# RWKV rounds of a hybrid decoder layer: three preparation steps asked for at other places of the round, and ten small operations per round moved to ScalarE

## The chip, the cores and the metric

The kernel runs on one core of a Trainium2 chip. A core has TensorE for matrix products (PE in the rows, with its weight loads as PEld), VectorE (DVE), ScalarE (ACT), GpSimd (POOL) and SyncE (SP), which issues the DMAs. Each engine works through its own queue in order; the engines wait for one another by semaphores. The metric is the device time of one execution in microseconds (us), the median of several runs; lower is better.

## The reference

A decoder layer for one sequence of 1024 positions and width 1024: RWKV-7 time mixing with 16 heads of 64, beside a dilated attention; then a cross-attention to 256 memory rows, a squared-ReLU MLP and norms. The change is in the RWKV part:

```
r, w, k, v, a_, b_ = ...            # projections of the normed input, mixed with the position before
for t in range(SEQ):                # per head, state is 64 x 64
    sa = state @ a_t
    state = state * w_t + outer(sa, b_t) + outer(v_t, k_t)
    y_t = state @ r_t
yn = groupnorm(y) * gn_w + gn_b
bonus = sum(r * k * r_k, per head) * v
out = (yn + bonus) * g
```

with `a_ = -kk`, `b_ = kk * a`, `k = p_k * (1 + (a - 1) * k_a)`, and `kk` the per-head normalised key.

## The kernel before

**Pairs, halves and chunks.** The 16 heads are worked off as 8 pairs p, a pair filling the 128 partitions. The 1024 positions are two halves of 512, a half is 8 chunks of 64 positions. Within a chunk the recurrence is put in closed form: a triangular system per chunk and head is solved, and what remains from chunk to chunk is a short scan over the state Z.

**Steps for one pair.** Each is a Python generator whose `yield`s cut it into small pieces:
- `proj`: the dense products (128x128 weights against 128x512 inputs, each value split into a high and a low part, three products per pair) that give r, k, v, evacuated by `shiftmix`.
- `prep_a` (L462): decay sums (L483), exponentials (L490, L491), the normalised key (L496 to L499), `ta` scaled by L502 on GpSimd, then k times ta (L503).
- `prep_b`: the operands `ar`, `bk` of the chunk products, and the chunk products themselves, masked into A (L546).
- `prep_d` (L550): `bk` times the decay of the chunk (L557, one instruction of 1024 elements), V centred and turned by TensorE into `pvt`, copied to UV by two half copies (L564 on ScalarE, L565 on VectorE), and b and k turned into BK (L571, L572).
- `prep_e` (L575): 64 small products of A with V, copied to UV (L582).
- `prep_c` (L585): the bonus: r times k (L588), the sum over a head by `block_sum` (L440, L442 and two products), times v (L594), and gn_b added by L595 on GpSimd.
- `solve` (L602): the triangular systems in blocks of 16: transposes (L613), then 14 times a product (L620) and a sum (L622) of tiny extent on VectorE, each needing the one before, and a last pair of transposes into DD (L633).
- `solve_pe` (L636): the joining products. From DD, four sets of small products double the solved blocks, from 16 to 32 to 64. Each set takes two PSUM banks and is read by VectorE or ScalarE (L648, L657, L666, L674, L684) before the next can begin.
- `post` (L688): the chunk matrices for the scan; its copies are L713 on ScalarE and L714 on VectorE for the two head halves of WT, L719 on ScalarE, and L726, ScalarE for the first head and VectorE for the second.
- `scan` (L745): chunk by chunk, a product into `pz`, Z made from it by VectorE (L760), a product into `pY`. `gnorm` (L765) follows.

All the small products' results lie in a pool of four PSUM banks (`pms`); the dense ones have two banks of their own.

**The order.** A round handles scan and group norm of pair p, the steps from prep_b to post of pair p+1, and proj and prep_a of pair p+2, with gate products as further dense work. `weave` merges the generators: every stream has a window (t0, t1) on a scale from 0 to 100 and a count n, and its pieces are written at t0 + (i + 1/2)(t1 - t0)/n, the earliest first. The windows of rounds 0 to 7 stand in W (L786), those of the round before them in W0. Where this text says "due", it means this place. The gate's dense pieces have dues 2.6 to 39.4, those of proj 43.2 to 98.8 in a round with both. From that written order the tile framework makes the queue of every engine when it compiles, along with all waits; the queue need not have the written order.

**The helper lines.** L125 is the product helper `mm`, so it is the line of nearly all small products: they are told apart by their tiles (`pz`, `pvt`, `psb`, `ps` for the joining products, `po` for those of prep_e and post). L143 to L145 are the dense products. L110 and L112 split the dense weights, on ScalarE and GpSimd.

Of the kernel before, what the change touches and what calls it, by code (L numbers as in the profile page):

```python
# [11 lines left out]
AF = mybir.ActivationFunctionType  # L12
ALU = mybir.AluOpType
# [28 lines left out]
def hybrid_layer(ctx, tc, x, mem, norm_mix_g, w_in, shift_mu, w0, w2, a0, a2, g2, k_k, k_a, r_k, gn_w, gn_b,  # L42
# [230 lines left out]
    with tc.tile_pool(name="ra", bufs=1, side="right", reuse_waits="tile") as ra, \  # L273
# [188 lines left out]
        def prep_a(p, half):  # L462
            d = st[p]
            hs = slice(half * H2, (half + 1) * H2)
            r, k, v = [d["rkv"][half].get(x) for x in "rkv"]
            wah = d["wa"]
            d[half] = e = {}
            psw = pms.tile([P, H2], F32, tag="m", name=nm("psw"))
            psa = pms.tile([P, H2], F32, tag="m", name=nm("psa"))
            mm(psw, wah[:, 0, :], WD[:, hs], True, False)  # L470
            mm(psa, wah[:, 1, :], AD[:, hs], True, False)
            mm(psw, wal[:, 0, :], WD[:, hs], False, True)
            mm(psa, wal[:, 1, :], AD[:, hs], False, True)
            sc = r3.tile([P, 2, H2], F32, tag="t4", name=nm("sc"), bufs=2)
            e["sg"], cs = sg, cs = sc[:, 0, :], sc[:, 1, :]
            nc.scalar.activation(sg, psw, AF.Tanh, bias=hw0[:, p:p + 1], scale=0.5)
            tt = r3.tile([P, 2, H2], F32, tag="t3", name=nm("ta"), bufs=2)
            ta, e["kk"] = tt[:, 0, :], tt[:, 1, :]
            sq = e["kk"]
            nc.scalar.activation(ta, psa, AF.Tanh, bias=ha0[:, p:p + 1], scale=0.5)  # L480
            yield
            nc.vector.tensor_scalar_add(sg, sg, 1.0)
            nc.vector.tensor_tensor_scan(cs, smask, sg, 0.0, op0=ALU.mult, op1=ALU.add)  # L483
            nc.scalar.activation(sq, k, AF.Square, scale=vc(V_KK, p))
            yield
            pss = pms.tile([P, H2], F32, tag="m", name=nm("pss"))
            block_sum(pss, sq)
            yield
            e["G"] = G = r3.tile([P, H2], F32, tag="t2", name=nm("G"), bufs=2)
            nc.scalar.activation(G, cs, AF.Exp, scale=-0.5 * CDEC)  # L490
            nc.scalar.activation(cs, cs, AF.Exp, scale=0.5 * CDEC)  # L491
            e["Gi"] = cs
            yield
            kk = sq
            nc.vector.tensor_scalar_max(kk, pss, 1e-24)
            nc.scalar.activation(kk, kk, AF.Ln, scale=2.0 ** 20)  # L496
            nc.scalar.activation(kk, kk, AF.Exp, bias=l2b, scale=-0.5)
            yield
            nc.vector.scalar_tensor_tensor(kk, k, vc(V_KK, p), kk, op0=ALU.mult, op1=ALU.mult)  # L499
            nc.vector.scalar_tensor_tensor(sg, ta, 1.0, cs, op0=ALU.add, op1=ALU.mult)  # L500
            yield
            nc.gpsimd.tensor_scalar(ta, ta, hka[:, p:p + 1], omhka[:, p:p + 1], op0=ALU.mult, op1=ALU.add)  # L502
            nc.vector.tensor_tensor(k, k, ta, op=ALU.mult)  # L503
            yield

# [44 lines left out]
        def prep_d(p, half):  # L550
            d = st[p]
            e = d[half]
            v = d["rkv"][half].get("v")
            bk, gC = e["bk"], e["gC"]
            us, vs = rows(half)

            nc.vector.tensor_tensor(bk, bk, gC.unsqueeze(3).broadcast_to([P, 8, 2, CH]), op=ALU.mult)  # L557
            e["UV"] = UV = rb.tile([P, 8, P], F32, tag="UV", name=nm("UV"), bufs=2)
            pvt = pms.tile([P, 4, P], F32, tag="m", name=nm("pvt"))
            for q in range(4):  # L560

                mm(pvt[:, q, :], v[:, q * P:(q + 1) * P], cen)
            uvp = UV.rearrange("p (q e) f -> p q e f", e=2)
            nc.scalar.copy(uvp[vs, :, 0, :], pvt[0:64])  # L564
            nc.vector.tensor_copy(uvp[vs, :, 1, :], pvt[64:128])  # L565
            yield
            e["BK"] = BK = rb.tile([P, 8, P], F32, tag="BK", name=nm("BK"), bufs=2)
            for q in range(2):
                pb = pms.tile([P, 4, P], F32, tag="m", name=nm("pb"))
                for i in range(4):  # L570
                    nc.tensor.transpose(pb[:, i, :], bk[:, q * 4 + i, :, :], ident)  # L571
                nc.scalar.copy(BK[:, q * 4:q * 4 + 4, :], pb)  # L572
                yield
# [11 lines left out]
        def prep_c(p, half):  # L585
            d = st[p]
            r, k, v = [d["rkv"][half].get(x) for x in "rkv"]
            nc.vector.scalar_tensor_tensor(r, r, vc(V_RK, p), k, op0=ALU.mult, op1=ALU.mult)  # L588
            yield
            psb = pms.tile([P, H2], F32, tag="m", name=nm("psb"))  # L590
            block_sum(psb, r)
            yield
            d[half]["bv"] = bv = rb.tile([P, H2], F32, tag="bv", name=nm("bv"), bufs=3)
            nc.vector.tensor_tensor(bv, psb, v, op=ALU.mult)  # L594
            nc.gpsimd.tensor_scalar(bv, bv, 1.0, vc(V_GB, p), op0=ALU.mult, op1=ALU.add)  # L595
            yield

        def quads():
# [89 lines left out]
        def post(p):  # L688


            d = st[p]
            Am = d["Am"]
            ar, UV, BK, gC = [[d[half][x] for half in range(2)] for x in ("ar", "UV", "BK", "gC")]
            d["S"] = rA.tile([P, 2, 4, 8, CH], F32, tag="A", name=nm("S"))
            St = d["S"]
            for f in range(2):
                nc.gpsimd.tensor_tensor(St[:, f, 0], id2.broadcast_to([P, 8, CH]), gC[f].broadcast_to([P, 8, CH]),
                                        op=ALU.mult)

            def us(f):  # L700
                return rows(f)[0]

            def am(f, c, h):
                return Am[us(f), 16 * f + 2 * c + h, 0:64]

            WT = []
            for f in range(2):
                pt = pms.tile([P, 4, P], F32, tag="m", name=nm("paT"))
                for q in range(4):
                    nc.tensor.transpose(pt[:, q, :], d[f]["ara"][:, 0, 2 * q:2 * q + 2, :], ident)  # L710
                WT.append(r3.tile([P, 8, P], F32, tag="bk", name=nm("WT"), bufs=2))
                wtp = WT[f][us(f)].rearrange("p (q e) f -> p q e f", e=2)
                nc.scalar.copy(wtp[:, :, 0, :], pt[0:64])  # L713
                nc.vector.tensor_copy(wtp[:, :, 1, :], pt[64:128])  # L714
            yield
            pu = four(lambda f, c, h, hh: (am(f, c, h), UV[f][us(f), c, hh]))
            for f in range(2):
                for hh in heads():
                    nc.scalar.copy(UV[f][us(f), :, hh], pu[f][hh])  # L719
            yield  # L720
            pw = four(lambda f, c, h, hh: (am(f, c, h), WT[f][us(f), c, hh]))

            for f in range(2):
                Wm = Am[us(f), 16 * f:16 * f + 16, 0:64].rearrange("p (c h) t -> p c h t", h=2)
                for h, hh in enumerate(heads()):
                    (nc.vector.tensor_copy if h else nc.scalar.copy)(Wm[:, :, h, :], pw[f][hh])  # L726
            yield
            ps = four(lambda f, c, h, hh: (BK[f][:, c, hh], UV[f][:, c, hh]))
            for f in range(2):
                nc.scalar.copy(St[:, f, 2], ps[f])  # L730
            yield
            ps = four(lambda f, c, h, hh: (am(f, c, h), BK[f][us(f), c, hh]))
            for f in range(2):
                nc.vector.tensor_tensor(St[:, f, 0], St[:, f, 0], ps[f], op=ALU.add)
            yield
            ps = four(lambda f, c, h, hh: (am(f, c, h), Am[us(f), 16 * f + 2 * c + h, 64:128]))
            for f in range(2):
                nc.vector.tensor_tensor(St[:, f, 1], ar[f][:, :, 1, :], ps[f], op=ALU.add)
            yield
            ps = four(lambda f, c, h, hh: (UV[f][:, c, hh], Am[:, 16 * f + 2 * c + h, 64:128]))  # L740
            for f in range(2):
                nc.scalar.copy(St[:, f, 3], ps[f])
            yield
# [21 lines left out]
        def gnorm(p, half):  # L765
# [17 lines left out]
            nc.sync.dma_start(yscr[p * P:(p + 1) * P, half * H2:(half + 1) * H2], y)  # L783
            yield

        W = dict(s0=(0, 22), s1=(23, 46), g0=(24, 36), g1=(47, 60), b0=(0, 10), b1=(7, 17), so=(17, 36), d0=(20, 30),  # L786
                 d1=(28, 38), sp=(36, 54), c0=(40, 44), c1=(45, 49), e=(37, 39), po=(56, 82), a0=(62, 78), a1=(76, 94))
        W0 = dict(b0=(20, 29), b1=(28, 37), so=(37, 52), d0=(38, 45), d1=(44, 51), sp=(52, 66), c0=(50, 54), c1=(54, 58),
                  e=(50, 52), po=(68, 90), a0=(68, 82), a1=(80, 96))
        GD = [4, 1, 1, 1, 1, 1, 1, 4, 2]  # L790
# [937 lines left out]
```

## Time and profile before

| | us |
|---|---|
| median of 3 runs (lowest, highest) | 2441.41 (2440.43, 2444.42) |
| the profiled execution | 2439.77 |
| its span, first instruction to last | 2438.1 |

The profile is of one execution on the chip. All places in the rows are us from the start of its span. The RWKV part lies before 915 us; the rounds with W begin at about 221, 319.4, 414.5, 509.1, 605.5, 702 and 796.5, and the last, with no preparation, at 883. A row of a timeline gives start, length, engine, line, operation, output tile <- input tiles, shapes, and how many instructions it merges; what stands in brackets is the idle time of that engine just before it and what ended it.

### The profile page before, as it was taken

What the parts mean: (1) busy time and instruction counts of PE and PEld (TensorE: products, weight loads), DVE (VectorE), ACT (ScalarE), POOL (GpSimd) and SP (SyncE); (2) the same over time, 40 slices, a digit from 0 to 9 for tenths busy, and PEclk for the clock granted to TensorE, in tenths of its full rate; (3) what the DMA queues carried; (4) which work ended last, traced back from release to release, by engine and by line L of the source; (5) the groups of instructions that cost most, each with busy time, mean ns of one, the idle gap of its engine ahead of it and who ended that gap; (6) DMA issues with size and microseconds to landing.
All of it is one profiled execution on the core that took longest, in us unless ns stands there. A gap on an engine that the chain in (4) does not pass through costs nothing. (4 is left out here: it accounts for less than half of the span.)

```text
span 2438.1 us, 46897 instructions
## 1 busy us (share of the span) xinstructions
PE 2304.0 (95%) x18645; PEld 1834.2 (75%) x18645; DVE 1589.6 (65%) x2723; ACT 1046.3 (43%) x2032; POOL 922.5 (38%) x749
## 2 busy tenths in 40 slices
PE   6999999999999999999999999999889999899997
PEld 5777777777777777777678888887668887677775
DVE  6638677686786612232555664456799999797785
ACT  5525645645456434334433454444422223344344
POOL 4321222222222222111245535324555554565664
PEclk9999999999999999999999999999999999999998
DMA  4221111111111123121355553223244445554342
GB/s 171 57 64 34 37 39 34 37 43 34 37 33 33 49 70 102 40 69 41 90 176 157 163 153 115 68 60 91 65 143 156 151 155 178 160 168 124 114 133 75
DMA packets 301618, 226.73 MB, mean 93 GB/s; under 512 B 16229, under 2 KB 252375, under 8 KB 301399
## 3 DMA queue, kind: packets, MB, share of 16 engines
q1 hardware_dynamic: 301111, 223.20, 30.2%
q8 instruction: 147, 2.41, 0.4%
q14 instruction: 72, 0.59, 0.1%
q10 hardware_dynamic: 288, 0.52, 0.1%
HBM read 169.99 MB, written 53.67 MB: 92 GB/s over the span
## 5 line engine op out<-in xcount | busy, mean ns | idle before, releaser
L143 PE MATMUL acc<-ah,wh 128*128 128x512 f32 (+1 forms) x1600 | 652.2, 408 | 11.3 <-DVE h L1048 3.0
L144 PE MATMUL acc<-al,wh 128*128 128x512 f32 (+1 forms) x1600 | 618.3, 386 | 3.2 <-POOL al L231 1.9
L145 PE MATMUL acc<-ah,wl 128*128 128x512 f32 (+1 forms) x1600 | 618.1, 386 | 0.4 <-POOL wl L112 0.4
L112 POOL TENSOR_TENSOR wl<-wr,wh 128x512 fp32r<-128x512 f32 x248 | 334.5, 1350 | 708.5 <-ACT wh L110 665.5
L143 PEld LDWEIGHTS acc<-ah,wh 128*128 128x128 f32 x1600 | 302.9, 189 | 79.3 <-issue 4.9
L145 PEld LDWEIGHTS acc<-ah,wl 128*128 128x128 f32 x1600 | 302.6, 189 | 62.4 <-POOL wl L112 0.8
L144 PEld LDWEIGHTS acc<-al,wh 128*128 128x128 f32 x1600 | 303.3, 190 | 51.2 <-POOL al L231 3.5
L1419 PE MATMUL ms<-ah,wh 128*128 128x512 f32 x768 | 308.8, 402 | 18.2 <-DVE sg L1429 12.4
L1420 PE MATMUL ms<-al,wh 128*128 128x512 f32 x768 | 308.6, 402 | 15.6 <-DVE al L129 10.3
L1421 PE MATMUL ms<-ah,wl 128*128 128x512 f32 x768 | 306.8, 400 | 1.0 <-POOL wl L1382 0.9
L110 ACT CAST wh<-wr 128x512 fp32r<-128x512 f32 (+1 forms) x296 | 179.5, 607 | 297.7 <-PE acc L144 183.8
L1382 POOL TENSOR_TENSOR wl<-ws,wh 128x512 fp32r<-128x512 f32 x128 | 185.2, 1450 | 155.9 <-ACT wh L1381 148.3
L1419 PEld LDWEIGHTS ms<-ah,wh 128*128 128x128 f32 x768 | 147.4, 192 | 56.0 <-ACT wh L1381 6.8
L1420 PEld LDWEIGHTS ms<-al,wh 128*128 128x128 f32 x768 | 147.6, 192 | 54.6 <-DVE al L129 16.0
L1382 POOL TENSOR_TENSOR wl<-sr,wh 128x512 fp32r<-128x512 f32 x96 | 141.6, 1476 | 119.8 <-ACT wh L1381 119.6
L1421 PEld LDWEIGHTS ms<-ah,wl 128*128 128x128 f32 x768 | 147.7, 192 | 35.0 <-POOL wl L1382 2.8
L1381 ACT CAST wh<-ws 128x512 fp32r<-128x512 f32 x128 | 79.2, 620 | 203.5 <-PE ms L1420 162.9
L1381 ACT CAST wh<-sr 128x512 fp32r<-128x512 f32 x96 | 59.2, 620 | 137.8 <-PE ms L1420 122.2
L937 DVE CUSTOM_DVE_ANT_0 sS<-pS,bias 128x128 f32<-128x128 f32 (+1 forms) x96 | 30.2, 349 | 114.6 <-PE pS L125 114.4
L129 DVE TENSOR_TENSOR al<-ur,ah 128x512 fp32r<-128x512 f32 x96 | 93.7, 1014 | 0.4 <-ACT ah L128 0.4
L128 ACT CAST ah<-ur 128x512 fp32r<-128x512 f32 x96 | 58.5, 620 | 61.2 <-DMA ur<-uscr 54.7
L942 ACT ACTIVATE sS<-sS,nm 128x128 f32<-128x128 f32 (+1 forms) x96 | 42.5, 443 | 75.1 <-DVE nm L940 72.0
(414 smaller groups left out, 3982.4 us busy)
## 6 DMA issues: line engine op xcount, KB each, us to landing
sr<-in_ffn_w_dram SPq DMA_DIRECT2D x134, 256.0 KB
wr<-in_w_in_dram SPq DMA_DIRECT2D x120, 256.0 KB
ur<-uscr SPq DMA_DIRECT2D x112, 256.0 KB
uscr<-sg SPq DMA_DIRECT2D x93, 256.0 KB
gtscr<-gt SPq DMA_DIRECT2D x32, 256.0 KB
g<-gtscr SPq DMA_DIRECT2D x32, 256.0 KB
wr<-in_p_rwkv_dram SPq DMA_DIRECT2D x32, 256.0 KB
wr<-in_w_out_dram SPq DMA_DIRECT2D x32, 256.0 KB
```

Source lines behind the costliest of these rows:

```text
L110: nc.scalar.copy(h, raw)
L112: lo_eng.tensor_tensor(l, raw, h.bitcast(F32), op=ALU.subtract)
L128: nc.scalar.copy(hi, src)
L129: (lo_eng or nc.vector).tensor_tensor(lo, src, hi.bitcast(F32), op=ALU.subtract)
L143: mms.append(nc.tensor.matmul(ps, h, ah, start=(k == 0), stop=False))
L144: mms.append(nc.tensor.matmul(ps, h, al, start=False, stop=False))
L145: mms.append(nc.tensor.matmul(ps, l, ah, start=False, stop=(k == len(acts) - 1)))
L1381: nc.scalar.copy(h, raw)
L1382: nc.gpsimd.tensor_tensor(l, raw, h.bitcast(F32), op=ALU.subtract)
L1419: nc.tensor.matmul(ps, h[:, k, :], ah, start=(k == 0), stop=False)
L1420: nc.tensor.matmul(ps, h[:, k, :], al, start=False, stop=False)
L1421: nc.tensor.matmul(ps, l[:, k, :], ah, start=False, stop=(k == 3))
```

## The change

- The windows in W: `d0` and `d1` (prep_d of the two halves), `e` (prep_e), `c0` and `c1` (prep_c) are given other places. W0 stays.
- Copies: L565, L714 and the second head's copy in L726 are issued on ScalarE in place of VectorE: two of each per round, six in all.
- Scalings: L502 and L595 are issued on ScalarE as an activation with scale and bias (or bias alone) in place of a tensor_scalar on GpSimd: two of each per round.

```
@@ prep_a
-            nc.gpsimd.tensor_scalar(ta, ta, hka[:, p:p + 1], omhka[:, p:p + 1], op0=ALU.mult, op1=ALU.add)
+            nc.scalar.activation(ta, ta, AF.Identity, bias=omhka[:, p:p + 1], scale=hka[:, p:p + 1])
@@ prep_d
             nc.scalar.copy(uvp[vs, :, 0, :], pvt[0:64])
-            nc.vector.tensor_copy(uvp[vs, :, 1, :], pvt[64:128])
+            nc.scalar.copy(uvp[vs, :, 1, :], pvt[64:128])
@@ prep_c
-            nc.gpsimd.tensor_scalar(bv, bv, 1.0, vc(V_GB, p), op0=ALU.mult, op1=ALU.add)
+            nc.scalar.activation(bv, bv, AF.Identity, bias=vc(V_GB, p))
@@ post
-                nc.vector.tensor_copy(wtp[:, :, 1, :], pt[64:128])
+                nc.scalar.copy(wtp[:, :, 1, :], pt[64:128])
...
-                    (nc.vector.tensor_copy if h else nc.scalar.copy)(Wm[:, :, h, :], pw[f][hh])
+                    nc.scalar.copy(Wm[:, :, h, :], pw[f][hh])
@@ windows
-        W = dict(s0=(0, 22), s1=(23, 46), g0=(24, 36), g1=(47, 60), b0=(0, 10), b1=(7, 17), so=(17, 36), d0=(20, 30),
-                 d1=(28, 38), sp=(36, 54), c0=(40, 44), c1=(45, 49), e=(37, 39), po=(56, 82), a0=(62, 78), a1=(76, 94))
+        W = dict(s0=(0, 22), s1=(23, 46), g0=(24, 36), g1=(47, 60), b0=(0, 10), b1=(7, 17), so=(17, 36), d0=(36, 44),
+                 d1=(42, 50), sp=(36, 54), c0=(50, 54), c1=(55, 59), e=(52, 54), po=(56, 82), a0=(62, 78), a1=(76, 94))
```

(s0, s1 scan; g0, g1 gnorm; b0, b1 prep_b; so solve; sp solve_pe; po post; a0, a1 prep_a.)

## Rows read from the trace of the kernel before

**Rows 1.** The page, busy us, share of the span, instructions.

```profile
PE 2304.0 (95%) x18645; PEld 1834.2 (75%) x18645; DVE 1589.6 (65%) x2723; ACT 1046.3 (43%) x2032; POOL 922.5 (38%) x749
```

**Rows 2.** Windows: stretch, length, then busy PE, PEld, DVE, ACT, POOL; granted clock.

```profile
414.50:509.10 94.60, 88.95 (x1400) 70.05 (x1400) 68.88 (x134) 50.22 (x77) 21.84 (x21) 1.00 0.13 37
...
796.50:883.00 86.50, 85.01 (x1386) 67.33 (x1388) 44.40 (x96) 35.14 (x56) 21.14 (x22) 1.00 0.18 54
```

**Rows 3.** Waits of PE, 221 to 796.5: total us, times, longest.

```profile
PE pz L125 <- DVE Z L760: 19.3, 23, 1.3
PE ps L125 <- issue: 6.1, 7, 1.2
```

**Rows 4.** Windows within the third round.

```profile
414.50:448.00 33.50, 29.98 (x286) 22.21 (x290) 29.90 (x73) 12.87 (x20) 6.37 (x8) 1.00 0.16 48
...
466.00:489.00 23.00, 22.43 (x390) 17.94 (x389) 12.86 (x22) 20.42 (x31) 5.69 (x5) 1.00 0.12 36
```

**Rows 5.** Timeline at the head of the third round.

```profile
412.84 1.77 DVE L588 SCALAR_TENSOR_TENSOR r<-r,vec,k 128x512 f32<-128x512 f32 x1
...
414.80 0.33 PE L125 MATMUL pz<-Z,S 64*64 64x64 f32 x4 [1.08 <-DVE Z L760]
```

**Rows 6.** Timeline, 434.8 to 440, all engines.

```profile
434.95 1.28 POOL L112 TENSOR_TENSOR wl<-wr,wh 128x512 fp32r<-128x512 f32 x1 [5.66 <-ACT wh L110]
435.02 1.28 DVE L622 TENSOR_TENSOR KX<-KX 128x50 f32<-128x50 f32 x1
...
436.59 0.22 DVE L622 TENSOR_TENSOR KX<-KX 128x54 f32<-128x54 f32 x1
...
437.09 0.69 DVE L565 COPY UV<-pvt 64x512 f32<-64x512 f32 x1
...
437.94 0.23 DVE L760 TENSOR_TENSOR Z<-pz,S 128x64 f32<-128x64 f32 x1
...
438.22 0.33 PE L125 MATMUL pz<-Z,S 64*64 64x64 f32 x4 [0.80 <-DVE Z L760]
```

**Rows 7.** Timeline of DVE, 430 to 448.8.

```profile
430.59 1.22 DVE L557 TENSOR_TENSOR bk<-bk,gC 128x1024 f32<-128x1024 f32 x1
431.84 0.69 DVE L565 COPY UV<-pvt 64x512 f32<-64x512 f32 x1
```

**Rows 8.** Timeline of PE, 446 to 455.

```profile
447.75 1.99 PE L125 MATMUL ps<-A,DD 32*32 32x64 f32 x128 [0.83 <-DVE DD L633]
449.67 1.16 PE L125 MATMUL po<-UV,A 64*64 64x64 f32 x64
450.76 0.41 PE L125 MATMUL ps<-DD,A 32*64 32x32 f32 x11
451.95 1.94 PE L125 MATMUL ps<-DD,A 32*64 32x32 f32 x117 [0.77 <-issue]
```

**Rows 9.** Groups of the third round: count, busy us, mean ns, idle before.

```profile
L582 ACT COPY UV<-po 64x512 f32<-64x512 f32 x4 | 2.3, 580 | 3.5 <-PE po L125 3.4
...
L125 PE MATMUL pvt<-cen,v 128*128 128x128 f32 x16 | 2.2, 281 | 0.0
...
L497 ACT ACTIVATE ta<-ta,l2b 128x512 f32<-128x512 f32 x2 | 1.4, 724 | 0.0
...
L565 DVE COPY UV<-pvt 64x512 f32<-64x512 f32 x2 | 1.4, 694 | 0.1
```

**Rows 10.** Timeline, 477.8 to 482, all engines.

```profile
478.79 1.17 ACT L726 COPY A<-po 64x512 f32<-64x512 f32 x2
...
479.39 1.42 DVE L726 COPY A<-po 64x512 f32<-64x512 f32 x2 [0.30 <-ACT A L726]
...
480.13 1.97 PE L125 MATMUL po<-UV,BK 128*64 128x64 f32 x60 [0.57 <-DVE A L726]
```

**Rows 11.** Timeline, 455 to 460, all engines.

```profile
455.72 0.68 DVE L442 TENSOR_TENSOR sl<-r,sp 128x512 fp32r<-128x512 f32 x1
455.92 1.04 POOL L595 TENSOR_SCALAR bv<-bv,vec 128x512 f32<-128x512 f32 x1 [7.07 <-DVE bv L594]
```

## What the change will do: the prediction

> **What bounds the kernel now.** I read the page's busy table first [rows 1]: TensorE is busy for 95% of the span and no other engine for more than 65%. Work taken from another engine is therefore worth only what it takes out of TensorE's idle time, so I next looked at the RWKV part by rounds [rows 2]. The reader is to see the difference of the first two numbers: in the third round TensorE does nothing for 94.60 - 88.95 = 5.65 us. Six rounds (221.0 to 796.5) repeat this pattern, some 34 us in all; a seventh, with other products, has 1.5 us. Nothing that the diff touches runs after that. So about 35 us, 1.5% of the kernel, is the most that better cover can give; TensorE's own work is the same before and after.
>
> Then TensorE's waits over the six rounds [rows 3]: 19.3 us for VectorE's state Z of the scan, and 6.1 us that no event ends ("issue"). In each round 0.83 us for DD, the output of the small solve [rows 8], and 0.57 us for VectorE's copy in L726 [rows 10] come on top. None of them is for ScalarE, which is busy 50 of 95 us [rows 2]. The stretch up to the joining products, 414.5 to 448 [rows 4], has 3.5 of the round's 5.65 idle us, and there VectorE is busy for 29.9 of 33.5 us.
>
> **What order means here.** The windows in W are due times in the written order. An engine's queue is not that order: L588, the first step of prep_c, is due at 45.7 of its round and ran at 412.84, ahead of the second scan product, which is due at 4.1 [rows 5]. So a due time is a preference among what is ready: it binds where an engine is full. I take TensorE to follow it closely, since it mostly has dense products ready, and VectorE in the stretch above only.
>
> **The change part by part.**
>
> *Windows.* prep_d goes from dues 20 to 38 to dues 36 to 50, prep_e from 38 to 53, prep_c from 40 to 49 to 50 to 59. On VectorE prep_d's L557 ran at 430.59, within a chain of tiny dependent steps (L620, L622) that leaves a slot after each [rows 7]; with a later due it still finds such a slot, so I leave it there, at no gain. Its other bound is that both L557 (1.22 each) leave the chain: DD 2.4 us earlier. On TensorE the V products (2.2 us a round [rows 9]) and as many for the turned b and k, about 4.5 us, slide behind the gate's dense blocks, which are due at 29 to 39, to shortly before DD. Mostly the order changes, not the amount done by then. Nothing that is moved issues a DMA, so no transfer passes another on a queue. Cost 0, hidden behind dense products; without that cover TensorE would stand for those 4.5 us.
>
> *The burst.* When DD comes, TensorE runs 128 small products, prep_e's 64 and then 128 more; after eleven of these it stands 0.77 us on "issue" [rows 8], and 6.1 over the six rounds [rows 3], 1.0 each. With prep_e due at 53 its 64 leave this burst. If the wait belongs to the length of the burst it goes; if it comes after so many instructions whatever they are, it stays. Bounds -1.0 and 0 a round; I take about the middle, -0.45.
>
> *L565 to ScalarE, two a round.* VectorE loses 2 x 0.69. The copy at 437.09 runs ahead of the Z of 437.94, for which TensorE stands 0.80 us [rows 6]; with the copy gone that Z can run 0.69 sooner: -0.7 a round. Bounds: 0, if the chain's own late steps, such as the 1.28 us L622 of the same rows, hold Z as long; -0.8, the whole wait. The other, at 431.84 [rows 7], stands before no wait that I count. The chain to DD is shorter by 2 x 0.69 = 1.4 us, more than the 0.83 wait for DD [rows 8]; but what TensorE does meanwhile is arranged against the same chain, so I take half, -0.4, between 0 and -0.83. What is late next are the other Z waits, 19.3/6 - 0.8 = 2.4 us a round, behind work of VectorE that the change leaves.
>
> *L714 and L726 to ScalarE, two each.* A copy of this shape costs 0.58 on ScalarE and 0.69 on VectorE [rows 9]. The two copies from one bank already run one behind the other: VectorE's L726 begins at 479.39, when ScalarE's first has ended, and TensorE waits 0.57 for it [rows 10]. On one engine the first bank is free after 2 x 0.58 = 1.17 in place of 0.58 + 0.69 = 1.27 us, and the second after 4 x 0.58 = 2.3 in place of 2.0 (478.79 to 479.39 + 1.42). That is -0.1 and +0.3: I take 0, between -0.57 and +0.3. Behind L714 I see no wait of TensorE. What queues behind ScalarE's longer run is L719 after L713, and L491, the casts of block_sum and L730 after L726. From 466 to 489 ScalarE is busy 20.4 of 23 us [rows 4]: it gets 2.3 us more there and runs that much late into the rest of the round, where it is busy 29.8 of 71.6 us. Dense products cover that; if they ran out, TensorE would stand for those 2.3 us.
>
> One rule speaks against these moves: the Trainium skill, "ScalarE: Activation LUTs", Rules for kernel authors, gives adds, multiplies and the like to VectorE and not to ScalarE. Where the source is a PSUM bank the rows say otherwise, 0.58 against 0.69 [rows 9], and the measurement decides; by the rule the six copies would add more work than they remove.
>
> *The scalings, two L502 and two L595 a round.* On GpSimd an L595 takes 1.04 [rows 11]; on ScalarE the nearest row, an activation from SBUF with a per-partition operand, takes 0.72 [rows 9]. No row has TensorE waiting for either, so 0. L502 now stands behind L497, the end of the chain that L499 waits for anyway, and L503 follows both. If it is put ahead of L497, L499 comes 0.7 late, and dense work covers that too. Does GpSimd's leaving free VectorE? Beside GpSimd's subtraction L112 a tiny L622 took 1.28 where the next such step takes 0.22 [rows 6]; beside the scaling L595 the subtraction L442 took 0.68 [rows 11], no more than a copy of that length. L112 stays. So 0, and -0.3 at most.
>
> By the Trainium skill, "SBUF — State Buffer", Who interferes with whom, a VectorE instruction with two SBUF inputs and a GpSimd instruction that reads SBUF shut each other out, and the second waits; L622 agrees, and L442, which began first, doesn't contradict. By that rule alone up to 4 x 1.04 = 4.2 us a round could come back to VectorE.
>
> *ScalarE as a whole* gets 6 x 0.58 + 4 x 0.72 = 6.4 us a round, and VectorE loses 6 x 0.69 = 4.2. A wait of TensorE on ScalarE is not in the trace. Bounds: 0, since ScalarE stays under 57 of 95 us; and 0.57, the size of the one bank wait there is, at each of the five joining hand-overs of two banks (L648 to L684), 2.85 a round. I take +0.4, near the lower end, where the rows are.
>
> **The sum.** -0.7 - 0.4 - 0.45 + 0 + 0.4 = -1.15 us a round; six rounds -6.9; the seventh, with a quarter of the idle time, -0.4. Together -7.3. The profiled execution took 2439.77 (span 2438.1 and 1.7 around it), so 2432.5 on its scale; the median of the runs is 1.6 above that execution, so 2434.1 on its scale. 0.2% is 4.9 us, about what a measurement of this kernel can tell from no change.
>
> **The rivals.**
>
> *The order does not change where it matters* (0.28). Ready work fills VectorE's slots whatever its due, and Z and DD are late because GpSimd's L112 stretches steps of the chain [rows 6], which stays. Then each wait reappears elsewhere and only some 0.3 us a round is left: 2439 to 2441. For it: L588 ran far from its due. Against: an L565 stands right before one of the waits.
>
> *A larger gain* (0.10). If both L565 and both L557 leave the chain and the burst is broken, the waits from 430 on go: 0.80 + 0.83 + 1.0 + 0.57 = 3.2 us a round, six times 19: about 2422. For it: VectorE is the only engine that TensorE waits for. Against: L557 finds its slots. By the Trainium skill, "SBUF — State Buffer", Who interferes with whom, the scalings' leaving GpSimd would push the same way.
>
> *Slower* (0.20). The four PSUM banks of one pool (pms) serve the joining products, which take two at a time, and also V, the turned b and k, prep_e and the bonus, now all due together. If a joining pair must wait for ScalarE to empty such a bank, all five hand-overs of a round wait 0.57: +2.85 a round less the 1.55 gained above, 7 times 1.3, +9, about 2450; with two copies ahead (1.2 each time) +31. It decides from the point at which a hand-over waits more than 0.31. For it: L726 shows that a bank wait reaches TensorE. Against: no wait on ScalarE so far, and dense products can stand in.
>
> **How the numbers follow.** The forecast, a gain of 5 to 14 us, has 0.42 and gives 2434; its own range is 2427 to 2436. Faster is that case and the large gain, 0.52; within 0.2% is the first rival, 0.28; slower is the last, 0.20. The range reaches into the large gain and past the lower end of the slower case: 2420 to 2452.
>
> **What would show it.** Right: the Z wait after L565 gone and the other Z waits still there; DD over 1 us earlier after the round's head; no "issue" wait after DD; VectorE near 64.7 and ScalarE near 56.6 us a round; TensorE idle about 4.5 us a round. Wrong: new waits of TensorE ended by ScalarE's copies, or Z waits of the same sum at other places.

## The result, and the profile after

The change made the kernel slower: 2475.55 us (four runs, 2465.05 to 2482.15) against 2440.92 (2439.53 to 2444.42), a ratio of 1.0141 [1.0120, 1.0162]. The forecast was 2434, range 2420 to 2452: wrong in sign and outside its range.

The profiled execution took 2465.05 us (span 2463.3). The median lies 10 us above it, and that goes with the clock: the four executions of 2465.05, 2469.42, 2481.67 and 2482.15 us had mean granted clocks of 0.985, 0.984, 0.978 and 0.974. In the profiled execution itself TensorE's granted clock stays at the upper level through all six rounds, so what that execution loses there is waits and busy time, and the lower level enters there only with the median.

The page's busy table of the kernel after, as [rows 1]:

```profile
PE 2309.9 (94%) x18645; PEld 1830.9 (74%) x18645; DVE 1556.2 (63%) x2675; ACT 1096.5 (45%) x2112; POOL 892.7 (36%) x717
```

The windows of its third and seventh round, as [rows 2]: stretch, length, busy PE, PEld, DVE, ACT, POOL, granted clock.

```profile
420.40:519.60 99.20, 90.35 (x1400) 70.10 (x1400) 63.60 (x128) 56.67 (x87) 17.95 (x17) 1.00 0.12 35
...
817.00:907.00 90.00, 87.68 (x1384) 68.46 (x1386) 41.58 (x90) 39.96 (x64) 18.98 (x20) 0.98 0.16 49
```

The third round is 4.6 us longer, with the same 1400 products at the same clock: TensorE idles 99.20 - 90.35 = 8.85 us in place of 5.65, and is busy 1.4 us longer. The seventh is 3.5 us longer. Outside the rounds the two kernels differ by some 3 us.

TensorE's waits over the six rounds of the kernel after, as [rows 3]:

```profile
PE pz L125 <- DVE Z L760: 18.8, 16, 1.8
PE ps L125 <- DVE DD L633: 12.9, 6, 2.2
PE po L125 <- ACT UV L719: 4.5, 6, 0.8
PE psb L125 <- ACT sp L440: 2.8, 6, 0.5
PE po L125 <- ACT WT L714: 2.6, 6, 0.5
PE psw L125 <- DVE S L734: 2.3, 6, 0.4
PE pY L125 <- DVE Z L760: 1.5, 6, 0.3
```

The "issue" wait of 6.1 us has shrunk to 0.4, the wait for L726's copy (3.4 us over the six rounds before) is gone, and Z costs about what it did. New are the waits that ScalarE's copies end (UV, WT), one for `sp` of the bonus, one for L734 and one of `pY` for Z; and the wait for DD has grown from 0.83 to 2.15 us a round. Those for DD, `sp` and `pY` came with the windows alone, as e1 will show. Their places on TensorE in the third round, from its timeline:

```profile
421.61 0.33 PE L125 MATMUL pz<-Z,S 64*64 64x64 f32 x4 [1.79 <-DVE Z L760]
...
453.02 1.99 PE L125 MATMUL ps<-A,DD 32*32 32x64 f32 x128 [2.15 <-DVE DD L633]
454.94 1.16 PE L125 MATMUL pvt<-cen,v 128*128 128x128 f32 x8
455.93 0.60 PE L571 MATMUL pb<-ident,bk 128*128 128x128 f32 x4
...
480.04 1.15 PE L125 MATMUL po<-UV,A 64*64 64x64 f32 x60 [0.43 <-ACT WT L714]
...
486.09 1.15 PE L125 MATMUL po<-WT,A 64*64 64x64 f32 x60 [0.75 <-ACT UV L719]
...
500.32 0.50 PE L125 MATMUL psw<-WD,wa 128*128 128x512 f32 x1 [0.40 <-DVE S L734]
```

Two of these waits fall within a group, after four of its 64 products, and then the group also takes longer: `po<-WT,A` was busy 1.2 us in the third round before and 1.5 after, `po<-UV,A` 2.3 and 2.6. A wait so costs some 0.3 us more than it shows; that is part of the 1.4.

What the copies meet on ScalarE, the same round's timeline of that engine:

```profile
478.82 0.58 ACT L713 COPY WT<-paT 64x512 f32<-64x512 f32 x1
...
479.40 0.58 ACT L714 COPY WT<-paT 64x512 f32<-64x512 f32 x1
...
483.67 2.37 ACT L719 COPY UV<-po 64x512 f32<-64x512 f32 x4
```

Four copies, L713 and L714 in turn, are one run from 478.82, and L719's (UV) come behind it and behind L595 and other work. TensorE waits until 480.04 for the L714 that begins at 479.40, and until 486.09 for the last of L719's.

### The profile page after: what moved, and what is told of

Read it like the earlier page. It is cut to its first block, busy times and chain, and to the rows that moved or that the text cites. A ratio compares the mean times of both kernels' runs of the same rounds, so it can differ in the third digit from the quotient of the medians.

```text
span 2463.3 us, 46923 instructions
## 1 busy us (share of the span) xinstructions
PE 2309.9 (94%) x18645; PEld 1830.9 (74%) x18645; DVE 1556.2 (63%) x2675; ACT 1096.5 (45%) x2112; POOL 892.7 (36%) x717
## 5 line engine op out<-in xcount | busy, mean ns | idle before, releaser
L112 POOL TENSOR_TENSOR wl<-wr,wh 128x512 fp32r<-128x512 f32 x248 | 332.6, 1343 | 881.7 <-ACT wh L110 819.0
L1419 PEld LDWEIGHTS ms<-ah,wh 128*128 128x128 f32 x768 | 146.3, 190 | 56.6 <-ACT ah L128 8.7
```

Of the source, the lines that this page charges most:

```text
L112: lo_eng.tensor_tensor(l, raw, h.bitcast(F32), op=ALU.subtract)
L1419: nc.tensor.matmul(ps, h[:, k, :], ah, start=(k == 0), stop=False)
```

## The experiments

Eighteen kernels. Each was timed beside the kernel before, which had medians of 2438.0 to 2441.4 us. "Rounds" is the windows view from the first scan product to that of the seventh round: its length, the busy time of TensorE, the difference of the two, the mean granted clock.

| run | what differs from the kernel before | us | ratio [95%] | rounds | busy | idle | clock |
|---|---|---|---|---|---|---|---|
| before | | 2440.92 | | 574.4 | 539.3 | 35.1 | 0.99 |
| after | all | 2475.55 | 1.0141 [1.0120, 1.0162] | 593.3 | 542.6 | 50.7 | 1.00 |
| e1_windows | windows | 2442.74 | 1.0008 [0.9994, 1.0022] | 573.1 | 536.5 | 36.7 | 1.00 |
| e2_copies | six copies | 2461.43 | 1.0086 [1.0069, 1.0103] | 591.2 | 550.1 | 41.1 | 0.97 |
| e3_scalings | L502, L595 | 2462.98 | 1.0093 [1.0075, 1.0110] | 594.1 | 546.3 | 47.8 | 0.99 |
| e4_de | windows d0, d1, e | 2444.32 | 1.0021 [1.0007, 1.0034] | 577.7 | 539.3 | 38.4 | 0.99 |
| e5_L502 | L502 | 2462.11 | 1.0084 [1.0058, 1.0110] | 593.3 | 547.8 | 45.5 | 0.98 |
| e6_L502_behind | L502, issued after L497 | 2443.08 | 1.0017 [1.0002, 1.0032] | 577.5 | 540.2 | 37.3 | 0.99 |
| e7_swap | L714, L726 to ScalarE, L719 to VectorE | 2468.36 | 1.0115 [1.0089, 1.0142] | 595.8 | 546.7 | 49.2 | 0.98 |
| e8_win565 | windows, L565 | 2444.23 | 1.0011 [0.9992, 1.0031] | 573.9 | 536.7 | 37.2 | 1.00 |
| e9_L714 | L714 | 2450.32 | 1.0036 [1.0023, 1.0049] | 580.3 | 539.8 | 40.5 | 0.99 |
| e10_L726 | L726 | 2458.56 | 1.0071 [1.0051, 1.0091] | 588.6 | 544.4 | 44.2 | 0.99 |
| e11_noload | no table loads | 2435.39 | 0.9982 [0.9968, 0.9996] | 563.5 | 534.3 | 29.2 | 1.00 |
| e12_copies_noload | six copies, no table loads | 2425.60 | 0.9939 [0.9922, 0.9956] | 560.5 | 534.9 | 25.6 | 0.99 |
| e13_after_behind | all, L502 issued after L497 | 2472.49 | 1.0133 [1.0111, 1.0155] | 598.6 | 548.2 | 50.4 | 0.99 |
| e14_ars | one root activation | 2427.68 | 0.9951 [0.9936, 0.9965] | 562.5 | 534.6 | 27.9 | 1.00 |
| e15_ars_copies | that, six copies | 2433.48 | 0.9971 [0.9955, 0.9987] | 567.2 | 536.7 | 30.5 | 0.99 |
| e16_after_ars | that, all of the change | 2460.73 | 1.0088 [1.0072, 1.0103] | 595.1 | 548.6 | 46.5 | 0.98 |
| e17_win_copies | all but L502, L595 | 2468.72 | 1.0113 [1.0095, 1.0130] | 604.0 | 551.4 | 52.6 | 0.98 |
| e18_win_scal565 | all but L714, L726 | 2469.13 | 1.0117 [1.0102, 1.0132] | 599.1 | 547.8 | 51.3 | 0.99 |

The expectations stand as they were written before each run, with the names that they give the theories. In short: by A the windows cost the time; by B ScalarE's load does, either by its place ahead of L497 (B1) or by its sum (B2); by C ScalarE is full between the joining products and L497, so that what is added there comes out late behind it.

### Which of the three parts: e1, e2, e3

e1 has the last hunk of the change's diff alone, e2 its lines L565, L714 and L726, e3 its lines L502 and L595:

```
e1: -  d0=(20, 30), d1=(28, 38), c0=(40, 44), c1=(45, 49), e=(37, 39)
e1: +  d0=(36, 44), d1=(42, 50), c0=(50, 54), c1=(55, 59), e=(52, 54)
e2: -  nc.vector.tensor_copy(...)    +  nc.scalar.copy(...)         (L565, L714, second head of L726)
e3: -  nc.gpsimd.tensor_scalar(...)  +  nc.scalar.activation(...)   (L502, L595)
```

> Only the new windows; all copies and scalings stay on their old engines. Theory A (the windows cost the time: TensorE has no work left before DD, since V and the turned b and k now stand behind the first joining product in its queue, and the dense products are cut into smaller pieces): about +18 us (2.7 us a round), the wait for DD 2 us or more a round against 0.83 before. Theory B (the windows are harmless, ScalarE's load costs the time): within 5 us of the kernel before, and the wait for DD near 0.8.

> Only the six copies on ScalarE, old windows, scalings on GpSimd. Theory A: between -5 and +3 us, the Z wait of 0.80 before which L565 stood is gone. Theory B: +10 us or more, with waits of TensorE ended by ScalarE's L714 and L719, 1.2 us a round or more.

> Only the two scalings on ScalarE, old windows, old copies. Theory A: +2 to +5 us, from L502 standing ahead of the table load of L497 so that the Z at the round's head comes 0.7 us later. Theory B: together with the copies all of the +25 to +34 us, here +10 or more.

The windows cost nothing. The copies and the scalings cost some 21 and 23 us, each by itself. All three times are those of theory B; but the wait for DD in e1, 2.1 us a round, is the one that theory A expected, and most of e2's wait is not at L714 and L719.

The windows' zero is a balance. TensorE's waits in e1:

```profile
PE pz L125 <- DVE Z L760: 14.7, 12, 1.5
PE ps L125 <- DVE DD L633: 12.8, 6, 2.2
...
PE psb L125 <- ACT sp L440: 2.3, 6, 0.4
PE po L125 <- DVE bv L594: 2.2, 6, 0.4
PE pY L125 <- DVE Z L760: 1.5, 6, 0.3
```

Against [rows 3] Z has lost 4.6 us and "issue" its 6.1; DD, 0.83 a round before [rows 8], has gained 7.8, and `psb`, `bv` and `pY` are new with 6.0. So the grown wait for DD came with the windows.

Where e2 loses, three timelines and one window say. First the kernel before, ScalarE, VectorE and TensorE about the first L497 of a pair:

```profile
484.63 1.28 ACT L497 ACT_TABLE_LOAD   x1
485.93 0.72 ACT L497 ACTIVATE ta<-ta,l2b 128x512 f32<-128x512 f32 x1
...
486.69 0.75 DVE L499 SCALAR_TENSOR_TENSOR ta<-k,vec,ta 128x512 f32<-128x512 f32 x1 [1.16 <-ACT ta L497]
487.54 0.69 DVE L503 TENSOR_TENSOR k<-k,ta 128x512 f32<-128x512 f32 x1
488.15 1.28 DVE L734 TENSOR_TENSOR S<-S,po 128x512 f32<-128x512 f32 x2
...
490.25 0.39 PE L125 MATMUL psw<-WD,wa 128*128 128x512 f32 x1
```

L497's table load stands on ScalarE behind L726, L496 and L730. VectorE's queue has L499, which needs L497, ahead of L734; and L734 empties the bank into which TensorE's next product in order, `psw`, writes. Before, `psw` comes 0.8 us after L734's end, without a wait. The same places in e2, one round on:

```profile
590.21 0.72 ACT L497 ACTIVATE ta<-ta,l2b 128x512 f32<-128x512 f32 x1
...
590.96 0.75 DVE L499 SCALAR_TENSOR_TENSOR ta<-k,vec,ta 128x512 f32<-128x512 f32 x1 [1.16 <-ACT ta L497]
591.82 1.59 DVE L503 TENSOR_TENSOR k<-k,ta 128x512 f32<-128x512 f32 x1
...
593.33 0.68 DVE L520 SCALAR_TENSOR_TENSOR bk<-ta,sc 128x512 f32<-128x512 f32 x1
...
593.93 1.27 DVE L734 TENSOR_TENSOR S<-S,po 128x512 f32<-128x512 f32 x2
...
591.52 1.34 POOL L112 TENSOR_TENSOR wl<-wr,wh 128x512 fp32r<-128x512 f32 x1 [4.79 <-ACT wh L110]
...
594.66 0.50 PE L125 MATMUL psw<-WD,wa 128*128 128x512 f32 x1 [1.42 <-DVE S L734]
...
596.37 0.63 PE L143 MATMUL acc<-ah,wh 128*128 128x512 f32 x1
```

TensorE reaches `psw` by 593.24 and stands 1.42 us for L734. The dense products behind it had their weights split by 592.86 (L112), and no copy out of a dense bank ran between; but they stand behind `psw` in the queue. That is what the prediction's "dense products cover that" overlooked: work that is ready covers a wait only if it stands ahead of it. L503 also took 1.59 in place of 0.69; GpSimd's L112 ran through most of it. And the framework put L520 (0.68) ahead of L734. Measured from the product group `po<-A` ahead of `psw`, L734 begins 2.9 us later than before: 1.4 us are L497's and L499's lateness, 0.9 L503's stretch, 0.7 L520. `psw` needs the first of L734's two instructions, which before was done some 1.4 us ahead of it, so L497's lateness alone would about have used up that room. In all six rounds of e2 the three come together.

Then the clock falls; the window of e2 that follows, granted clock behind the five busy times:

```profile
595.50:599.50 4.00, 4.00 (x23) 2.72 (x24) 3.93 (x9) 1.60 (x3) 0.00 (x0) 0.57 0.00 0
```

TensorE had waited 0.60, 0.67 and 1.42 us within 17 us; from about 595.7 it works at the lower of its two levels, 1.2 GHz, and a dense product takes 0.63 us in place of 0.39. Over the rounds e2 idles 6.0 us more than before, but is busy 10.8 us more, at a mean clock of 0.97: most of its loss is this. The same `psw` wait comes in each of the six rounds, but a fall follows it within 5 us in only three; what decides is not shown.

### Which copy: e9, e10, e8, e4

```
e9:  + nc.scalar.copy(wtp[:, :, 1, :], pt[64:128])         (L714 alone)
e10: + nc.scalar.copy(Wm[:, :, h, :], pw[f][hh])           (L726 alone)
e8:  + windows, nc.scalar.copy(uvp[vs, :, 1, :], pvt[64:128])   (L565)
e4:  + d0=(36, 44), d1=(42, 50), e=(52, 54)                (c0, c1 as before)
```

> Only L714 on ScalarE, all else as before. Theory C (ScalarE is full between the joining products and L497; what is added there comes out at L719, L497 and, through VectorE's queue, at L734's bank): about half of the three copies' cost, +8 to +13 us, with waits for L719 and L734. If the place is L726: within 4 us.

> Only the second copy of L726 on ScalarE, all else as before. Theory C: about half of the three copies' cost, +8 to +13 us, with the wait for L734. If the place is L714: within 4 us.

> The new windows and L565 on ScalarE; L714, L726 and the scalings as before. These two copies lie in the joining stretch, where ScalarE is idle more than half of the time. Theory C: within 5 us of the windows alone (2442.7). If any copy on ScalarE costs: +4 us or more against it.

> Only the windows of prep_d and prep_e; prep_c keeps its old windows, all engines as before. Theory A: nearly all of what the windows alone cost, +14 to +18 us, with the long wait for DD. If the bonus (prep_c) is what collides with the joining products: within 5 us of the kernel before.

L565 adds nothing to the windows: 1.0011 beside 1.0008. L714 costs 0.36%: UV of L719, behind it on ScalarE, now ends a wait of 3.7 us in six rounds, and L726's goes from 3.4 to 5.0; the wait for L734 that theory C expected is not there. L726 costs 0.71%: the `psw` wait of 1.4 us each round (8.5 in six) is all there. The copies that come last before L497 cost most. The two together cost more by themselves (1.07%) than the six copies of e2 (0.86%). c0 and c1 can stay or go: e4 is at 1.0021 [1.0007, 1.0034], and the two intervals overlap; theory A's +14 us is not there.

### Is it the copies' own engine: e7

```
- for hh in heads(): nc.scalar.copy(UV[f][us(f), :, hh], pu[f][hh])          (L719)
+ for hh in heads(): nc.vector.tensor_copy(UV[f][us(f), :, hh], pu[f][hh])
```

with L714 and L726 on ScalarE, so that it has as many copies as before.

> L714 and the second copy of L726 on ScalarE as in the change, and in exchange all four copies of L719 on VectorE; L565 and the scalings as before. ScalarE has the same load in the stretch after the joining products as before. Theory C (the copies cost because ScalarE is full between the joining products and L497, so that all behind comes late and a bank read by VectorE's L734 is given back late): within 6 us of the kernel before, the wait of psw for L734 gone. If it is the place of L714 and L726 themselves: +10 us or more.

It came out no better than the six copies of e2, 1.0115 beside 1.0086, and by its time against theory C. The `psw` wait came once in place of six times, as C had it, but TensorE waits now for VectorE's L719; e7's waits and VectorE's timeline:

```profile
PE po L125 <- DVE UV L719: 14.9, 12, 1.4
```

```profile
584.17 0.75 DVE L320 SCALAR_TENSOR_TENSOR k<-acc,vec,k 128x511 f32<-128x511 f32 x1 [2.14 <-ACT k L319]
584.84 1.20 DVE L324 TENSOR_TENSOR k<-k,carry 128x1 f32<-128x1 f32 x1
...
585.96 2.81 DVE L719 COPY UV<-po 64x512 f32<-64x512 f32 x4
```

VectorE stood 2.14 us for L319, which ScalarE reached behind its four copies of WT, and L719 stood behind that, with an L324 between that took 1.20 us in place of 0.15 while GpSimd's L112 ran. The lateness passed from one engine's queue into the other's.

### Which scaling, and its place: e5, e6, e13

```
e5:  + nc.scalar.activation(ta, ta, AF.Identity, bias=omhka[:, p:p + 1], scale=hka[:, p:p + 1])
e6:  + key = nc.scalar.activation(kk, kk, AF.Exp, bias=l2b, scale=-0.5)      (L497)
     + with tc.issue_after(key.ins): the line of e5
e13: the whole change with e6's two lines
```

> Only L502 on ScalarE; L595 stays on GpSimd, all else as before. In ScalarE's queue L502 now stands ahead of the table load of L497 in both halves of a round. Theory B1 (what costs is a ScalarE operation put ahead of L497, whose result L499 and all of VectorE behind it wait for): +15 to +23 us, nearly all of the scalings' cost, the Z waits near 4 us a round. Theory B2 (any added ScalarE time costs, by its sum): half of the scalings' cost, about +11.

> Only L502 on ScalarE, as in the run before, but held behind L497 in ScalarE's queue, so that L497 comes no later than before. Theory B1: within 6 us of the kernel before. Theory B2: the same as with L502 ahead of it.

> The whole change, but L502 held behind L497 in ScalarE's queue. If L502's place is a part of its own: 8 to 16 us less than the whole change, and the Z wait at the round's head back from 1.8 to 1.1 us. If the copies alone set L497's time in the full change: no more than 4 us less, the Z wait at the head as in the whole change.

L502 alone is nearly all of the scalings' 0.93%. ScalarE's timeline in e5, with L502 where the framework put it, and in e6, where it is held behind L497:

```profile
508.43 0.80 ACT L502 ACTIVATE ta<-ta,vx 128x512 f32<-128x512 f32 x1
509.25 1.28 ACT L497 ACT_TABLE_LOAD   x1
510.54 0.72 ACT L497 ACTIVATE ta<-ta,l2b 128x512 f32<-128x512 f32 x1
```

```profile
500.29 1.28 ACT L497 ACT_TABLE_LOAD   x1
501.58 0.72 ACT L497 ACTIVATE ta<-ta,l2b 128x512 f32<-128x512 f32 x1
502.21 0.80 ACT L503 ACTIVATE ta<-ta,vx 128x512 f32<-128x512 f32 x1
```

(e6's lines are one later.) Ahead of L497 it delays L499, and VectorE's queue has L499, L503, L516 to L521 and L588 ahead of the Z with which the next round's scan goes on. That Z wait is 1.79 us in e5, and in this round the clock falls within 5 us; a window of e5 from there on:

```profile
516.80:521.00 4.20, 3.31 (x34) 2.67 (x35) 2.37 (x8) 0.72 (x2) 1.26 (x1) 0.81 0.26 69
```

e6 does the same work behind L497 and costs 0.17% in place of 0.84%: the place costs, not the work. How it costs is less plain. Over six rounds the Z waits fall only from 24.4 to 22.9 us (19.3 before), since in e6 VectorE takes 6.7 us from L499 to that Z where in e5 it takes 5.7; the Z wait is still 1.61 us. TensorE's idle time falls by 8.2 us, and its busy time by 7.6, about half of which the clock can account for: 20.5 us of e5's rounds are at the lower level, 13.7 of e6's. In e6 the clock held after this wait, but in two other rounds it fell after one like it (1.61 and 1.70 us).

In the whole change the place is worth nothing: e13 is at 1.0133 beside 1.0141. Its longest Z wait is even 2.5 us. By its Z wait this expectation was missed; by its time it is in the second branch. VectorE's timeline in e13 shows where the gain went:

```profile
524.01 1.25 DVE L519 TENSOR_SCALAR ar<-ta 128x8 f32<-128x8 f32 x1
```

Measured from the next round's first scan product, L499 does come 0.4 us sooner than in the kernel after, but this tiny instruction (L518 there) takes 1.25 us in place of 0.17, so that VectorE needs 6.65 us from L499 to that Z in place of 5.7. GpSimd's L112 runs beside it; no run took that away.

### What makes L497 late: e11, e12

Ln (L496, L778) and Exp (L497, L779) load their tables in turn, eight loads of 1.283 us a round, 10.3 us of ScalarE's 50. Putting Identity in Ln's place takes the loads away:

```
- nc.scalar.activation(kk, kk, AF.Ln, scale=2.0 ** 20)
+ nc.scalar.activation(kk, kk, AF.Identity, scale=2.0 ** 20)      (and at L778 likewise)
```

> The kernel before with the two logarithms (L496, L778) replaced by an identity, so that the activation table is not changed any more in the rounds: 8 table loads of 1.28 us a round fall away. The values behind it are not the reference's. This is the baseline for the next run. Theory C: faster, by 5 us or more, because L497 comes sooner. If ScalarE is not what matters: within 5 us of the kernel before.

> The run before with the six copies on ScalarE (again identities in place of the two logarithms). Theory C: ScalarE has 10.3 us a round less to do, so the copies cost nothing against that baseline: within 6 us of it. If the copies cost by their own latency, whatever ScalarE's load: +15 to +21 us against it, as without the change of the logarithms.

e11, 0.9982, lies on the line between its two theories. Without the loads the six copies gain 9.8 us (2435.39 to 2425.60) where with them they cost some 21. The timelines of ScalarE and VectorE in e12 at the place shown for e2:

```profile
474.18 0.62 ACT L496 ACTIVATE ta<-ta 128x512 f32<-128x512 f32 x1
474.83 0.72 ACT L497 ACTIVATE ta<-ta,l2b 128x512 f32<-128x512 f32 x1
...
479.05 1.27 DVE L734 TENSOR_TENSOR S<-S,po 128x512 f32<-128x512 f32 x2
```

L497 follows L496 at once, and no `psw` waits. So the copies are worth what was hoped of them on a ScalarE with 10 us a round more room, part of it just ahead of L497. Neither e11 nor e12 computes the reference.

### A version that beats both: e14, e15, e16

A single activation gives the reciprocal root, so that Ln and Exp are not needed:

```
- nc.scalar.activation(kk, kk, AF.Ln, scale=2.0 ** 20)
- nc.scalar.activation(kk, kk, AF.Exp, bias=l2b, scale=-0.5)
+ nc.scalar.activation(kk, kk, AF.Abs_reciprocal_sqrt)      (and at L778, L779 likewise)
```

> The kernel before with one activation, the reciprocal square root, in place of a logarithm and an exponential, at L496/L497 and at L778/L779: ScalarE has 2.9 us a round less to do and the table load that used to stand between the two now follows the result. Theory C (what counts is how soon L497's result is there): faster by 5 to 15 us. If the load of ScalarE does not matter here: within 5 us.

> The run before with the six copies on ScalarE, old windows, scalings on GpSimd. Theory C: the copies cost nothing any more or gain, -8 to +5 us against that run. If they cost by their own latency: +15 us or more against it.

> The whole change with the reciprocal square root. Theory C: most of the change's +25 to +34 us is gone, within 8 us of the kernel before or faster; what stays is L502 ahead of the one activation that L499 waits for. If the cost is not ScalarE's lateness: still +20 us or more.

e14, the kernel before with this alone, is the fastest of those that compute all of the reference: 2427.68, 0.9951 [0.9936, 0.9965]. With the copies it is 5.8 us slower than e14, just outside theory C's -8 to +5, with the whole change 33 us slower. The last expectation was missed by theory C, and the time, +21 us against the kernel before, is the other branch's; the timelines of ScalarE and TensorE in e16 show a reason that I had not thought of:

```profile
585.57 2.37 ACT L718 COPY UV<-po 64x512 f32<-64x512 f32 x4
587.96 1.28 ACT L476 ACT_TABLE_LOAD   x1
...
592.23 2.35 ACT L725 COPY A<-po 64x512 f32<-64x512 f32 x4
...
593.44 3.26 PE L125 MATMUL po<-UV,BK 128*64 128x64 f32 x60 [1.98 <-ACT A L725]
```

The new activation has a table of its own, and L476 now loads another: the loads are as many as before, and only their places changed. (e16's lines are one earlier.) In e14 that is a gain, since one load and one activation leave the way to L499; but one load now stands between the two runs of copies, and in e16 TensorE waits 1.98 us for A behind it, 11.9 in six rounds. Its wait for DD is longer still, 17.3 us in six rounds, and was not followed up.

### Pairs of parts: e17, e18

```
e17: the change without the two lines L502 and L595
e18: the change without the two lines L714 and L726
```

> The whole change less the scalings: new windows and six copies, L502 and L595 back on GpSimd. If the copies of post carry the whole change's cost: +19 us or more against the kernel before. If the scalings do, which add 3 us of ScalarE time a round: within 6 us of it. If they share it: +8 to +16 us.

> The whole change less L714 and the second copy of L726: new windows, L565 and both scalings on ScalarE. If the copies of post carry the cost: within 6 us of the kernel before. If the scalings do: +19 us or more. If they share it: +8 to +16 us.

Both are at 1.011 to 1.012, some 30 us: each meets its "+19 us or more", so on the new windows the copies alone or the scalings alone are enough for most of the loss, and the second of them adds little. Windows (0.08%), copies (0.86%) and scalings (0.93%) would sum to 1.87%; together they cost 1.41%. That fits a shared cause, since by the timelines both make L497's result late, but it does not show one. One reason why they do not add up can be read: with the scalings added, L112 begins behind L503 and no longer ahead of it, L503 is back at 0.69 us, and the `psw` wait falls from 7.0 us over six rounds in e17 to 2.3 in the kernel after.

## Why the prediction was wrong, step by step

- **Windows, "Cost 0, hidden behind dense products":** right in total (e1), not in its parts. I had the V products and the turned b and k slide "to shortly before DD". A part went behind the first joining products (454.94, 455.93), so TensorE reaches DD sooner than DD comes: its wait for DD rose from 0.83 us a round to 2.15. The L557, which were to stay where they were, did move ahead of the chain to DD.
- **The burst, -0.45:** the right direction, and the full gain of 1.0 was the truth: the "issue" wait of the joining products went from 6.1 us to 0.4 after, and is not among e1's waits.
- **L565, -0.7, and DD, -0.4:** L565 gave nothing (e8 beside e1). DD did come sooner, but not by L565: 453.02 - 417.62 = 35.4 us after the round's first scan product in place of 447.75 - 411.67 = 36.1, and already 34.2 with the windows alone (e1). The wait for it still rose by 1.3, because the work ahead of it on TensorE had left.
- **L714 and L726, "I take 0, between -0.57 and +0.3":** here the prediction failed. It saw no wait behind L714, named the 2.3 us by which ScalarE would run late and wrote "dense products cover that". They don't, where they stand behind the product that waits: in e2 and in e10 `psw` stands 1.4 us a round. 0.36% and 0.71% by themselves are 8.8 and 17.3 us, or 1.3 and 2.5 a round over seven rounds.
- **The scalings, 0, "dense work covers that too":** the same mistake at L499. It is the step with the plainest warning: the text saw that L502 might be put ahead of L497, and then priced it at nothing. It cost 0.84% by itself, and 0.17% once it stood behind L497. Its length was a small miss besides: L502 takes 0.80 us on ScalarE, where 0.72 was taken.
- **ScalarE as a whole, +0.4:** I looked for the price at the joining hand-overs (L648 to L684), and none of the new waits is there; those that ScalarE's added work brought are at WT, UV and, through VectorE's queue, L734 and Z. The slower rival had the right sign and the wrong place.
- **The counts:** ScalarE 56.67 us in the third round for 56.6, VectorE 63.6 for 64.7. TensorE's idle time is 8.85 us for 4.5. (The "34 us" of idle time in six rounds is 35.1 in the table's row; nothing hangs on it.) How much work each engine gets was never the question.
- **Not in the sum at all:** the clock. Waits of one or two us had no price beyond their length. Of e2's loss more than half is time at the lower level; in the kernel after it is no more than the 10 us or so from the profiled execution to the median.

The Trainium skill, "ScalarE: Activation LUTs", Rules for kernel authors, had spoken against these moves by giving adds, multiplies and the like to VectorE; copies, to which the prediction applied it, are not in its list. Its direction held, but not by the duration of the copies: the copies take 0.58 us on ScalarE and 0.69 on VectorE [rows 9], and in e12 they gain.

**Open:** how far the wait for DD and the low clock in e16 belong together; what decides whether the clock falls after a short wait; and what lengthens L503, L516 and L518 in some rounds: GpSimd's L112 runs beside them, but no run took it away. Nor did any run hold L520 behind L734, so the price of the framework's new order by itself is not shown.

## What to carry to other kernels

Before an engine is called free because it is busy for half of the time, follow the queue from the moved instruction to the next result that another engine waits for, and then that engine's queue to the next product of TensorE: each engine works off its queue in order, and ready work behind a waiting instruction is no cover. Price a move by what stands right behind it, not by the engine's share; hold a moved instruction behind the one that others wait for, as e6 does. Look for table loads on that path first: here taking an activation and its load out of it gained 0.49%, while the ten moves cost 1.4%.

## What the runs showed of the hardware

- The granted clock fell to 0.5 (1.2 GHz) after waits of TensorE that were short by themselves: 0.60, 0.67 and 1.42 us within 17 us in e2, 1.79 in e5. It did not do so every time: the `psw` wait of 1.4 us in e2 was followed by a fall in three rounds of six, and the Z wait of e6 by a fall after 1.61 us at 412.6 and 1.70 us at 699.5, but by none after 1.61 us at 509.3.
- Ln and Exp loaded a table each, in turn, 1.283 us every time; with one reciprocal-root activation in their place half of the loads moved to L476 and L399 and they did not become fewer: 48 in the six rounds of e14 as before.
- VectorE's L503 took 0.69 us in every round of the kernel before, of e6 and of e9, and in the first halves of the kernel after, where GpSimd's L112 had not begun ahead of it, and 1.58 to 1.66 us in the first halves of e2, e5, e10 and e17, where L112 had begun 0.2 to 0.3 us before. The other way round, L112 took 1.28 us where it began behind L503's end, and 1.42 to 1.58 where L503 had begun ahead of it and still ran. No run took L112 away.
